# FFN up projection: one pass of 512 prompt tokens per Strassen half, sample tokens as separate float32 products

## The chip, the core and the metric

The kernel runs on one core of a Trainium2 chip. The metric is the device time of one execution in microseconds (us), the median of several runs. The core has five engines with instruction queues of their own: PE (matrix products; its weight loads are listed as PEld), DVE (vectors), ACT (activations, copies, casts), POOL (general) and SP (which here only issues DMA transfers). They meet through semaphores.

## The reference

The program is one step of an encoder layer for 1024 prompt tokens (one new stream) and 32 sample tokens (one running stream): a mixer of three head groups, its output projection, and a feed-forward network with a causal convolution. The change concerns the last:

```python
def conv_ffn(xn, buf, w_up, conv_w, conv_b, w_down):      # D_MODEL 1024, D_FF 2816, FFN_CONV 3
    up = xn @ w_up                                        # (T, 1024) @ (1024, 5632)
    up, buf = causal_dwconv(up, buf, conv_w, conv_b)      # per channel: b + sum_j up[t - 2 + j] * w[j]
    gate, val = jnp.split(up, 2, axis=-1)
    return (jax.nn.gelu(gate, approximate=True) * val) @ w_down, buf
```

It is run for the prompt with an empty buffer and for the samples with a cache of the last two rows of `up` (`cache_ffn_conv`, 2 x 5632); both return the last two rows of their `up` (outputs `p_fc` and `q_fc`). All is float32.

## The kernel before

The kernel goes through its stages in one program: mixer projections and heads, output projection, up projection, down projection, tail. A tile scheduler sets the order on each engine from the order of the code, from priorities (`tc.high_priority`) and from explicit rules (`tc.issue_after`). Names in traces are those of tiles without their number.

A float32 product is made of three products of reduced type (`mm3`, L100 to 103): each operand is split into a high half (`...h`, a cast on ACT) and a low half (`...l`, the difference on DVE), and PE adds high x high (L101), low x high (L102) and high x low (L103) in PSUM.

The up projection uses one level of Strassen's method in Winograd's form. The 1024 inputs are cut in two (four k tiles of 128 each), the tokens in two halves of 512 columns, and the 5632 outputs into 22 pairs of 128 rows (`f` and `22+f`). Seven products p1 to p7 make one pair: `PROD` names their operands, of which those on the weights' side (A11, A12, A22, S1 to S4) are made anew for each f in `up_operands`, and those on the activations' side (B11, B21, B22, T1 to T4) are made once in `col_operands` and stay in SBUF. One product is four k tiles times three matmuls, 12 matmuls; seven are 84.

A Strassen half holds 512 prompt tokens and 16 of the samples, 528 columns. PSUM's bank holds 512, so `SUBS` cuts it in two passes, s=0 of 272 columns and s=1 of 256: 168 matmuls per f. `up_block` issues one pass. It is a generator, advanced by `up_all`: p2 into bank `puy`; p1 into `pux`, p5 into `puw`, p4 into `puz`; p6 on top of `pux` and p3 on top of `puw`; p7 on top of `pux`. Between them ACT copies `pux` or `puw` out (`keep`, L1345: c1, c5, c6, c7) and DVE adds such a copy and a bank into the conv's input `uu` (`out`, L1350), in pieces given by `PIECES`. `uu` has 1060 columns: the two prompt halves with the samples between them, and gaps of two columns for the conv's history.

`up_finish` runs for the f before: POOL fills gaps, samples' cache and halo (L1403 to 1406), ACT applies the middle tap and the bias (L1407), DVE the other two taps, ACT the GELU, DVE the product, and SP stores the result to `h_d` in DRAM (L1413). `up_raw` (L1292) loads the weights `wu<j>r` of the next f. In the entry to this stage, f=0's first pass is interleaved with the output projection's last two tiles (`zp`, tiles 6 and 7), whose normalized and transposed result (`z`, `fxt`, `xg`) is the last part of T1 and B22 of the second half.

The down projection reads `h_d` tiles back as `ht` and multiplies the prompt's part by Strassen as well. The samples are multiplied apart in `sample_products` (L1530): float32 products without split, 32 sample columns as weights and 512 columns of the down weights moving, into one quarter of the partitions of a bank each.

## Time and profile before

| | us |
|---|---|
| runs | 1359.47, 1356.77, 1357.68; median 1357.68 |
| span of the profiled execution | 1355.3 |
| PE busy | 1310.8 |
| DVE, ACT, POOL busy | 1025.2, 709.8, 317.6 |

The profile gives the span from the first to the last instruction. What lies around the span is not in it; the three runs without profile are 1.5 to 4.2 us above it, the median 2.4. In the rows of a timeline the first number is the start and the second the duration, both in us; of pipelined matmuls the durations overlap, so the rate is read from the distance of the starts. A bracket at the end gives the idle time ahead of an instruction and what ended it.

### The profile page before, as it was taken

The page shows a single profiled execution, that of the slowest core. Times are in us where ns is not written, and L with a number is a line of the kernel's source. Part 1 is how long each engine was busy: PE and PEld are TensorE (multiplying, and loading weights), DVE is VectorE, ACT ScalarE, POOL GpSimd, SP SyncE. Part 2 cuts the span into 40 slices and gives each one's busy share as a digit, 9 for nine tenths or more (in the row PEclk, how much of TensorE's full clock was granted, in tenths as well). Part 3 has the DMA queues.
Part 4 walks back from the last instruction along what each step waited for, and adds up shares of the span by engine and source line. Part 5 has one row for each costly group of instructions (what it writes and reads, how often), then busy time and mean ns, then how long its engine had stood idle before and what let it go on. Part 6 is the DMA issues. An engine that isn't in the chain of part 4 may idle for free.

```text
span 1355.3 us, 29229 instructions
## 1 busy us (share of the span) xinstructions
PE 1310.8 (97%) x11472; PEld 1196.7 (88%) x11472; DVE 1025.2 (76%) x1921; ACT 709.8 (52%) x1362; POOL 317.6 (23%) x530
## 2 busy tenths in 40 slices
PE   6999999999999999999999999999999999999997
PEld 5999889998888887767899999999999996678885
DVE  5795649768598678876998888888888876499566
ACT  5555556555574555435654554545554545454552
POOL 4532303135032254213211212111111110010005
PEclk9999999999998989989999999999999999999998
DMA  9799778886879963454315457536455239645435
GB/s 342 241 358 363 265 244 258 278 281 211 292 230 308 336 201 125 142 182 103 128 48 188 134 133 189 134 111 180 120 147 154 82 127 397 254 161 146 141 102 124
DMA packets 126881, 269.72 MB, mean 199 GB/s; under 512 B 24167, under 2 KB 59143, under 8 KB 126663
## 3 DMA queue, kind: packets, MB, share of 16 engines
q1 hardware_dynamic: 113111, 244.78, 53.2%
q0 software_dynamic: 9120, 18.62, 7.3%
q10 hardware_dynamic: 4512, 4.46, 1.0%
q8 instruction: 90, 1.47, 0.5%
q14 instruction: 48, 0.39, 0.1%
HBM read 206.72 MB, written 86.18 MB: 216 GB/s over the span
## 4 chain that ended last, share of the span: by engine, by line
PE 63%; DVE 5%; DMA 3%; ACT 3%; issue 2%; POOL 1%; SPq 0%; DVEq 0%; POOLq 0%; ACTq 0%
PE pux L103 5%; PE pux L102 5%; PE pux L101 5%; PE puw L101 3%; PE puw L103 3%; PE puw L102 3%; PE q L101 3%; PE q L102 3%; PE q L103 3%; PE x L101 2%; PE x L102 2%; PE x L103 2%; PE puz L103 2%; PE puz L101 2%; PE puz L102 2%
## 5 line engine op out<-in xcount | busy, mean ns | idle before, releaser
L1409 DVE SCALAR_TENSOR_TENSOR y<-uu,fconv_sb,y 128x1060 f32<-128x1060 f32 x88 | 116.2, 1320 | 36.8 <-ACT y L1407 36.2
L1345 ACT COPY c<-pux 128x272 f32<-128x272 f32 (+1 forms) x132 | 49.3, 375 | 50.5 <-PE pux L103 49.8
L1407 ACT ACTIVATE y<-uu,fconv_sb 128x1060 f32<-128x1060 f32 x44 | 56.1, 1275 | 8.5 <-POOL uu L1403 7.8
L101 PE MATMUL pv<-wt_0h,xh 128*128 128x256 f32 (+1 forms) x192 | 56.3, 293 | 3.6 <-DVE xl L334 1.6
L103 PE MATMUL zp<-woh,cl 128*128 128x512 f32 (+1 forms) x144 | 57.7, 401 | 1.5 <-DVE cl L1106 1.5
L1406 POOL COPY fhalo<-uu 128x2 f32<-128x2 f32 x44 | 16.6, 376 | 180.7 <-DVE uu L1350 180.6
L101 PE MATMUL zp<-woh,ch 128*128 128x512 f32 (+1 forms) x144 | 57.8, 410 | 0.8 <-ACT ch L1105 0.8
L102 PE MATMUL zp<-wol,ch 128*128 128x512 f32 (+1 forms) x144 | 57.9, 402 | 0.0
L103 PE MATMUL pv<-wt_1h,xl 128*128 128x256 f32 (+1 forms) x192 | 55.1, 287 | 0.0
L103 PE MATMUL pv<-wt_0h,xl 128*128 128x256 f32 (+1 forms) x192 | 55.0, 286 | 0.0
L102 PE MATMUL pv<-wt_0l,xh 128*128 128x256 f32 (+1 forms) x192 | 54.8, 286 | 0.0
L101 PE MATMUL pv<-wt_1h,xh 128*128 128x256 f32 (+1 forms) x192 | 54.7, 285 | 0.0
L102 PE MATMUL pv<-wt_1l,xh 128*128 128x256 f32 (+1 forms) x192 | 54.4, 283 | 0.0
L1585 POOL TENSOR_TENSOR gss<-gss 128x1 f32<-128x1 f32 (+1 forms) x9 | 8.2, 906 | 185.0 <-ACT gjk L1578 185.0
L221 POOL TENSOR_SCALAR hrs<-hss 128x5 f32<-128x5 f32 (+3 forms) x27 | 10.1, 375 | 176.5 <-DVE hss L1015 172.6
L831 DVE COPY_PREDICATED P<-masks_sb,sc 128x352 f32<-128x352 int32 (+3 forms) x53 | 37.9, 715 | 5.9 <-PE sc L744 5.0
L101 PEld LDWEIGHTS pv<-wt_0h,xh 128*128 128x128 f32 x192 | 36.4, 190 | 5.3 <-DVE xl L334 2.1
L1403 POOL COPY uu<-uu 128x2 f32<-128x2 f32 x44 | 28.0, 637 | 38.8 <-DVE uu L1350 37.8
L101 PEld LDWEIGHTS pv<-wt_1h,xh 128*128 128x128 f32 x192 | 36.2, 189 | 0.7 <-issue 0.6
L222 POOL TENSOR_TENSOR hrs<-hrs,mhalf 128x5 f32<-128x5 f32 (+3 forms) x27 | 36.2, 1341 | 2.2
L103 PEld LDWEIGHTS pv<-wt_0h,xl 128*128 128x128 f32 x192 | 36.5, 190 | 0.2
L102 PEld LDWEIGHTS pv<-wt_0l,xh 128*128 128x128 f32 x192 | 36.5, 190 | 0.1
(1743 smaller groups left out, 5321.0 us busy)
## 6 DMA issues: line engine op xcount, KB each, us to landing
wrP<-in_w_dn SPq DMA_DIRECT2D x27, 512.0 KB, 4.4
h_d<-y SPq DMA_DIRECT2D x22, 530.0 KB, 3.7
ht<-h_d SPq DMA_DIRECT2D x22, 530.0 KB, 10.5
wt_0r<-in_w_tok SPq DMA_DIRECT2D x21, 512.0 KB, 5.7
wt_1r<-in_w_tok SPq DMA_DIRECT2D x21, 512.0 KB, 6.3
ws_d<-in_w_dn POOLq DMA_DIRECT2D x20, 512.0 KB, 8.9
wrP<-ws_d SPq DMA_DIRECT2D x20, 512.0 KB, 4.0
wt_0l<-lt_d SPq DMA_DIRECT2D x14, 512.0 KB, 4.5
```

Source lines behind the costliest of these rows:

```text
L101: pe.matmul(ps, lh[0], rh[0], start=first, stop=False, **kw)
L102: pe.matmul(ps, lh[0], rh[1], start=False, stop=False, **kw)
L103: return pe.matmul(ps, lh[1], rh[0], start=False, stop=last, **kw)
L221: pool.tensor_scalar(out, ss, 1.0 / width, eps, op0=ALU.mult, op1=ALU.add)
L222: pool.tensor_tensor(out, out, mhalf[:n, :cols], op=ALU.pow)
L831: dve.copy_predicated(dst, mk.broadcast_to([n, 11, *mk.shape[2:]]), src)
L1345: kept[name] = act.copy(t, ps)
L1403: pool.tensor_copy(u[:, GAP_P:GAP_P + 2], u[:, GAP_S - 2:GAP_S])
L1406: behind["POOL"] = pool.tensor_copy(fhalo[:, j, :], u[:, NCOL - 2:NCOL])
L1407: act.activation(y, u, AF.Identity, scale=fconv[:, j, 2:3], bias=fconv[:, j, 3:4])
L1409: dve.scalar_tensor_tensor(y, uu[i][:, s:s + NCOL], fconv[:, j, s:s + 1], y, op0=ALU.mult, op1=ALU.add)
L1585: pool.tensor_tensor(ss[:n, 0:1], ss[:n, 2:3], ss[:n, 3:4], op=ALU.add)
```

## The change

- `SUBS`, `PIECES` and the gaps go. Only f=0 still runs in two passes (0 and 1, both of 256 columns, as the second needs the last out-projection tiles). From f=1 to f=21 there is one pass of 512 columns, so 84 matmuls instead of 168. The activation halves (`X`) are one set of tiles, 512 columns wide; T2, T3 and T4 live in pool `px1`, the rest in `px0`. In the last f the order of products is p2, p5, p1, p3, p6, p4, p7 in code.
- `uu`, `y`, `h_d` and `ht` have 1024 columns. `out` is one DVE sum of 512. Of the POOL copies only `fhalo` remains.
- The samples get a second layout of the up weights, `w_us`, made on the host: 24 rounds (3 groups of columns x 8 k tiles), each [128, 4 (in the last group 3 used), 512]. `up_samples` is a generator that `up_all` advances behind p4 of f=1 and later. A round is 4 or 3 float32 matmuls (weights 32 sample columns, moving 512 columns of `wus`) into quarters of one bank `us`. After 8 rounds ACT copies the bank to SBUF, PE transposes it in four steps, and ACT puts the parts into `smp_u` [128, 44, 34]. Behind the last group POOL does the conv of the samples (12 operations of 128x704), ACT the GELU, POOL the product into `smp_h`, which `sample_products` uses in place of `ht`.
- `wus` holds two rounds (1 MB each) in the SBUF place of `xg0`; a round's reload is issued when it has been used. The samples' cache is read straight into `smp_u` (pieces of 8 bytes) and `q_fc` written from it.
- The program is built with a DMA scratch of 4096 bytes instead of the default.

```diff
-SUBS = [(0, 272), (272, 256)]
+NU = 2 * NF
+UGROUPS = [(0, 4), (4, 4), (8, 3)]
...
     def halves(name, src):
             if name not in res:
-                p = pool_[name in ("T2", "T3")]
-                h = p.tile([128, 4, n], F32R, name=f"{name}h{s}")
...
+                p = pool_[name in ("T2", "T4", "T3")]
+                res[name] = tuple(p.tile([128, 4, 512], F32R, name=f"{name}{x}") for x in "hl")
+            h, l = (t[:, :, at] for t in res[name])
...
     def up_block(pw_, f, s, W, X, uu, own={}):
-        n = SUBS[s][1]
+        at = slice(0, 512) if s is None else slice(256 * s, 256 * s + 256)
+        n = at.stop - at.start
...
         def out(i, j, x, ps, op=ALU.add):
-            for (a0, a1, c) in PIECES[j, s]:
-                dve.tensor_tensor(uu[i][:, 2 + c:2 + c + a1 - a0], x[:, a0:a1], ps[:, a0:a1], op=op)
+            c = 2 + 512 * j + at.start
+            dve.tensor_tensor(uu[i][:, c:c + n], x, ps, op=op)
...
-            pool.tensor_copy(u[:, GAP_P:GAP_P + 2], u[:, GAP_S - 2:GAP_S])
-            pool.tensor_copy(u[:, GAP_S:GAP_S + 2], fcache[:, j, :])
-            pool.tensor_copy(fcache[:, j, :], u[:, GAP_P - 2:GAP_P])
...
+    def up_samples():
...
+        def load(i):
+            if i < len(ROUNDS):
+                g, k = ROUNDS[i]
+                nq = UGROUPS[g][1]
+                sp.dma_start(wus[:, i % 2, :nq], a["w_us"][8 * g + k, :, :nq])
+        smp_u = own.tile([128, NU, 2 + DEC], F32, name="smp_u")
+        sp.dma_start(smp_u[:, :, 0:2], a["fcache"])
...
+        sp.dma_start(smp_x, xn_d[:, :, SEQ:])
...
+        for g, (c0, nq) in enumerate(UGROUPS):
+            ps = psf.tile([128, 512], F32, tag="sx", name=f"us{g}", bufs=1)
+            for k in range(8):
+                for q in range(nq):
+                    pe.matmul(ps[DEC * q:DEC * q + DEC], smp_x[:, k, :], wus[:, i % 2, q, :], start=k == 0, stop=k == 7)
+                load(i + 2)
+                i += 1
+                if k < 7:
+                    yield
+            m = DEC * nq
+            us = own.tile([128, 512], F32, tag="us", name=f"usr{g}", bufs=1)
+            act.copy(us[:m], ps[:m])
+            yield
+            tp = psb.tile([128, 4, 128], F32, tag="big", name=f"ust{g}", bufs=3)
+            for b in range(4):
+                pe.transpose(tp[:, b, :m], us[:m, 128 * b:128 * b + 128], ident[:m, :m])
+            for b in range(4):
+                act.copy(smp_u[:, 4 * c0 + b:4 * (c0 + nq):4, 2:2 + DEC], tp[:, b, :m].rearrange("p (q t) -> p q t", t=DEC))
...
     def up_all(pw_, W0, X, uus, py, freed, ahead, begun):
-            for s in range(2):
+            for s in (0, 1) if f == 0 else (None,):
...
                 yield
+                while f and n_rounds < f * 28 // 18:
+                    next(rounds, None)
+                    n_rounds += 1
                 next(blk)
...
-                    pe.matmul(ps[r:r + DEC], hts[q + NP * k][:, SMP:SMP + DEC], wraws["P2" if k else "P1", q][:, j],
+                    pe.matmul(ps[r:r + DEC], smp_h[:, q + NP * k, :], wraws["P2" if k else "P1", q][:, j],
```

On PE, in the steady part of the stage, before (f=4; p4 ends in `puz4_0`, p6 follows; further on p3 ends and the second pass begins with `puy4_1`):

```order
L102 MATMUL puz4_0_10020<-T4l0_8847,A22_4h_9841 128x272
L103 MATMUL puz4_0_10020<-T4h0_8846,A22_4h_9841 128x272
L101 MATMUL pux4_0_10018<-T2h0_8842,S2_4h_9850 128x272
L102 MATMUL pux4_0_10018<-T2l0_8843,S2_4h_9850 128x272
...
L103 MATMUL puw4_0_10019<-B22h0_8835,S4_4h_9854 128x272
L101 MATMUL puy4_1_10115<-B21h1_8948,A12_4h_9835 128x256
```

The same place on PE after (`us0` is the bank of the first group of columns; x8 are two rounds of four):

```order
L89 MATMUL puz4_None_9687<-T4l_8928,A22_4h_9585 128x512
L90 MATMUL puz4_None_9687<-T4h_8927,A22_4h_9585 128x512
L1433 MATMUL us0_9448<-wus_8941,smp_x_9300 32x512 x8
L88 MATMUL pux4_None_9685<-T2h_8923,S2_4h_9594 128x512
L89 MATMUL pux4_None_9685<-T2l_8924,S2_4h_9594 128x512
```

The rounds stand between p4 and p6, and there is no second pass. Such an insertion comes once in each f from 1 to 17, 17 in all; f=1, 4, 6, 8, 9, 11, 13 and 15 hold two rounds, the others one, and one round is cut into 3 matmuls in f=2 and 1 in f=3. The three groups of transposes stand ahead of the rounds of f=7 and f=12 and shortly behind the round of f=17.

On ACT, in the entry, before (`xg` filled from the last transposes, then casts of the first half, with the out-projection's `z6` and its sums between):

```order
L1258 CAST B11h_8813<-xg_6906 128x1088
L1210 ACTIVATE xg_6906<-fxt_8705,gcols_sb 128x128 x4
L1210 ACTIVATE xg_6906<-fxt_8714,gcols_sb 128x128 x4
L1130 ACTIVATE z_8747,oss_8632<-zp_8633 128x512
L1130 ACTIVATE z_8747,oss_8632<-zp_8634 128x512
L1258 CAST B22h_8835<-xg_6906 128x1088
L1258 CAST T1h_8831<-xg_6906 128x1088
```

The same place on ACT after:

```order
L1117 ACTIVATE z_8743,oss_8632<-zp_8633 128x512
L1117 ACTIVATE z_8743,oss_8632<-zp_8634 128x512
L1242 CAST B21h<-xg_6885 128x4x256
L1242 CAST B11h<-xg_6885 128x4x256
L1242 CAST B22h<-xg_6885 128x4x256
L1118 COPY z_8743<-zp_8633 128x512
```

The casts of B21 and B11 of the first half have moved behind the filling of `xg` and the two activations of `z6`.

On SP, ahead of the weights of f=2, before:

```order
L1185 DMA x_d<-xr_8752 128x1024
L1805 DMA fconv_sb<-in_fconv 128x176
L1807 DMA fcache_sb<-in_fcache 128x88
L1185 DMA x_d<-xr_8807 128x1024
L1292 DMA wu2r<-in_w_up 128x1024
L1292 DMA wu24r<-in_w_up 128x1024
```

The same place on SP after:

```order
L1172 DMA x_d<-xr_8803 128x1024
L1418 DMA wus<-in_w_us 128x2048 x2
L1421 DMA smp_u<-in_fcache 128x44x2
L1424 DMA smp_x<-xn_d 128x8x32
L1276 DMA wu2r<-in_w_up 128x1024
L1276 DMA wu24r<-in_w_up 128x1024
L1418 DMA wus<-in_w_us 128x2048 x2
L1407 DMA h_d<-y_9211 128x1024
```

Four loads for the samples now stand ahead of `wu2r`, and the reload of the first two rounds stands ahead of the store of the first `h`.

More of the change, by code (lines that the diff above doesn't have):

```diff
@@ L1323, in body, with product @@
     done = [None]
-    def product(ps, p, W, X, first, last):
+    def product(ps, p, W, X, first, last, at):
         (wh, wl), (xh, xl) = W[PROD[p][0]], X[PROD[p][1]]
@@ L1864, in body @@
     p4s.close()
+    pgs.close()
 def _layout(i):
```

209 lines of the change are left out of this document (117 added, 92 removed).

## The prediction

> **What bounds the kernel now.** I read the page's busy times first, then the chain that ended last, then a table of windows by stage, and last the timelines of the matmuls themselves.
>
> ```profile
> PE 1310.8 (97%) x11472; PEld 1196.7 (88%) x11472; DVE 1025.2 (76%) x1921; ACT 709.8 (52%) x1362; POOL 317.6 (23%) x530
> PE 63%; DVE 5%; DMA 3%; ACT 3%; issue 2%; POOL 1%; SPq 0%; DVEq 0%; POOLq 0%; ACTq 0%
> ...
> 657.50:690.00 32.50, 28.80 (x211) 28.22 (x210) 30.62 (x46) 20.64 (x32) 9.54 (x15) 0.89 0.18 58
> 700.00:800.00 100.00, 100.00 (x820) 100.00 (x819) 84.08 (x141) 51.08 (x88) 16.58 (x45) 1.00 0.52 151
> 1140.00:1200.00 60.00, 58.19 (x271) 39.17 (x270) 31.60 (x51) 25.54 (x49) 0.00 (x0) 1.00 0.76 288
> ```
>
> The window rows give bounds and length, then busy time of PE, PEld, DVE, ACT and POOL, the granted clock, the DMA share and GB/s. In the steady up projection (700 to 800) PE is busy for the whole window at full clock. No other engine is: DVE has 84.08, ACT 51.08, DMA 0.52. So a microsecond taken from PE's issue there is a microsecond off the end, until DVE's share binds. The entry into the stage (657.5 to 690) is another matter: PE has 28.80 of 32.50, the clock is 0.89, and DVE with 30.62 is the fullest engine.
>
> **Term 1, long passes.** Per f-tile, 84 matmuls of 272 columns and 84 of 256 become 84 of 512; this holds for f=1 to 21. First the rate before, by one POOL instruction that comes once per f-tile, by the change-over of shapes in the last f-tile, and then the rate of 512-column matmuls of the same three-pass form in the down projection (one P7h cast per 12 of them) and in the output projection.
>
> ```profile
> 727.93 0.58 POOL L1406 COPY fhalo<-uu 128x2 f32<-128x2 f32 x1 [4.96 <-DVE uu L1350]
> ...
> 789.54 0.58 POOL L1406 COPY fhalo<-uu 128x2 f32<-128x2 f32 x1 [4.98 <-DVE uu L1350]
> ...
> 1108.26 0.29 PE L101 MATMUL pux<-T3h,S_21h 128*128 128x272 f32 x1
> ...
> 1109.77 0.28 PE L101 MATMUL pux<-B11h,A_21h 128*128 128x256 f32 x1
> ...
> 1111.20 0.28 PE L101 MATMUL puw<-T1h,S_21h 128*128 128x256 f32 x1
> ...
> 1296.35 0.62 ACT L107 CAST P7h<-ht 128x512 fp32r<-128x512 f32 x1 [1.58 <-PE x L103]
> ...
> 1301.79 0.62 ACT L107 CAST P7h<-ht 128x512 fp32r<-128x512 f32 x1 [1.58 <-PE x L103]
> ...
> 651.64 0.39 PE L101 MATMUL zp<-woh,ch 128*128 128x512 f32 x1
> ...
> 653.00 0.39 PE L101 MATMUL zp<-woh,ch 128*128 128x512 f32 x1
> ```
>
> Three f-tiles take 789.54 − 727.93 = 61.61 us, so one takes 20.54, and a pair (272 and 256) 20.54/84 = 244.5 ns. By shape: 12 of 272 take 1109.77 − 1108.26 = 1.51, or 125.8 ns each; 12 of 256 take 1.43, or 119.2. The 512 form takes (1301.79 − 1296.35)/24 = 226.7 ns, and (653.00 − 651.64)/6 = 226.7 in the output projection. Sixteen columns cost 6.6 ns, so 256 cost about 106 and each matmul carries some 13 ns whatever its width; the long pass pays that once instead of twice and drops 16 columns. Saved: 244.5 − 226.7 = 17.8 ns a pair, 1.495 us an f-tile, **−31.4 us** for 21. For f=0 the passes stay at two but the first loses 16 columns: 84 × 6.6 ns = **−0.55**.
>
> The Trainium skill ("TensorE: Matmul & The Clock Gate", section "Back-to-back issue gap") puts an isolated warm matmul at N/2.4 + 2.5 ns. By it 272 and 256 would take 225.0 ns and 512 would take 215.8, a saving of 9.2 ns a pair and 16.2 us in all. The trace's 119.2 for 256 columns lies 10 ns above that rule's 109.2, and here the measurement decides.
>
> **Term 2, sample rounds.** The 32 sample tokens leave the passes and come back as 24 rounds of 4 (16 rounds) or 3 (8 rounds) float32 matmuls, 32 sample columns stationary, 512 weight columns moving, each into its quarter of PSUM's partitions. The down projection has exactly this form, four at a time (x8, as each float32 matmul leaves two records) and once two at a time (x4).
>
> ```profile
> 1125.85 0.39 PE L103 MATMUL q<-P2w,P2h 128*128 128x512 f32 x1
> 1126.17 1.07 PE L1530 MATMUL s<-wrP,ht 128*32 128x512 f32 x8
> 1127.17 0.50 PE L101 MATMUL q<-P2w,P2h 128*128 128x512 f32 x1
> 1127.51 0.39 PE L102 MATMUL q<-P2w,P2h 128*128 128x512 f32 x1
> ...
> 1194.07 0.39 PE L103 MATMUL x<-P1w,P1h 128*128 128x512 f32 x1
> 1194.39 1.05 PE L1530 MATMUL s<-wrP,ht 128*32 128x512 f32 x4
> 1195.37 0.50 PE L101 MATMUL q<-P4w,P4h 128*128 128x512 f32 x1
> 1195.71 0.39 PE L102 MATMUL q<-P4w,P4h 128*128 128x512 f32 x1
> ```
>
> From the last ordinary matmul to the second one behind the group it is 1127.51 − 1125.85 = 1.66; two ordinary intervals would be 0.45, so a group of four costs 1.21 us. A group of two costs 1195.71 − 1194.07 − 0.45 = 1.19: the quarters run beside each other, and three cost what four do. Of the 1.21, 1.00 (1126.17 to 1127.17) is the round and 0.2 the change of form on both sides. PE's order has 17 insertions, always behind product p4; eight hold two rounds, one round is cut into 3 and 1 over two f-tiles, so there are 25 round times. 17 × 1.20 + 8 × 1.00 = **+28.4**. No row shows two rounds in a row on the same quarters. Ends: 25 × 1.00 = 25.0 if the changes of form hide; 25 × 1.21 = 30.3 if a second round pays its own. I take 28.4, since the change of form is at the border.
>
> **Term 3, transposes.** Each of three groups is brought back with four 128x128 float32 transposes. The nearest row is such a group inside the output projection:
>
> ```profile
> 640.50 0.39 PE L103 MATMUL zp<-woh,cl 128*128 128x512 f32 x1
> 640.73 0.60 PE L1101 MATMUL ctp<-ident,cat 128*128 128x128 f32 x4
> 641.09 0.48 PE L101 MATMUL zp<-woh,ch 128*128 128x512 f32 x1
> 641.40 0.40 PE L102 MATMUL zp<-wol,ch 128*128 128x512 f32 x1
> ```
>
> 641.40 − 640.50 − 0.45 = 0.45, times three is **+1.35**.
>
> **Term 4, the entry.** Here the order of the activation halves changes.
>
> ```profile
> 676.05 0.58 PE L101 MATMUL puw<-T1h,S_0h 128*128 128x256 f32 x1 [2.93 <-ACT T1h L1258]
> 676.43 0.43 PE L101 MATMUL pux<-B11h,A_1h 128*128 128x272 f32 x1
> ...
> 679.15 0.41 PE L102 MATMUL puw<-T1l,S_0h 128*128 128x256 f32 x1
> ...
> 681.50 0.41 PE L101 MATMUL pux<-T2h,S_0h 128*128 128x256 f32 x1
> ...
> 682.68 0.39 PE L101 MATMUL puw<-B22h,S_0h 128*128 128x256 f32 x1 [0.77 <-ACT c L1345]
> ...
> 693.74 0.33 SPq L1292 DMA_DIRECT2D wu2r<-in_w_up  x1
> ...
> 697.35 0.62 ACT L107 CAST A_2h<-wu2r 128x512 fp32r<-128x512 f32 x1 [0.73 <-DMA wu2r<-in_w_up]
> ```
>
> Before, PE loses 2.93 and 0.77 to waits, and behind the first it runs slow: 12 of 272 take 2.72 instead of 1.51 and 11 of 256 take 2.35 instead of 1.31, another 2.25. Together 5.95 us. The last prompt tile's normalization on ACT and POOL, with DVE's copies and sums, feeds T1h there, and nothing of that chain is shortened. After, ACT runs the out-projection's z6 ahead of the first half's B21h and B11h, T2 and T4 of that half come later on DVE, and p6 of f=0 has to wait for its T2 low half; against that, p1 of f=1 fills the gap before T1 with 12 matmuls of 512 instead of 272 (2.72 against 1.51 at full clock). Walked with the durations of these rows: T1's second half comes about 1 us later (677 instead of 676.05), because z7's chain starts 1 us later on ACT; the filler does 1.2 us more work ahead of it; the rest of f=0 behind T1 is the same work at the same slow start. That is −0.2. The wait of p6 for T2 is about 2.7 us at a place where PE ran on before; the wait for T1 comes after it and would have been idle anyway, so it swallows that but for 0 to 2 us. I take **+0.4** in all, near the low end, as the swallowing is exact if T1 really ends last. The outer ends are −5.95 (all of the loss gone) and +5.2 (one more wait of 2.93 with its slow 2.25).
>
> **What I cost at nothing.** Per f-tile DVE has 0.84 × 20.54 = 17.3 us and ACT 10.5; both fit into the 19.04 us of 84 × 226.7 ns even unchanged, and they shrink (four 512-wide sums for twelve pieces, 66 copies for 132, y of 1024 for 1060). If DVE did not keep up, PSUM banks would come free late and PE would wait at p6. The three gap copies on POOL go; the samples' convolution there is 13 instructions of 704 columns, due four f-tiles (76 us) after the last round, which covers even 5 us each. The second weight layout brings 16 × 1.05 + 8 × 0.79 = 23 MB in 330 us, 70 GB/s on 151: a share near 0.76, as the 1140 window has with PE at 58.19 of 60. Each reload waits in SP's queue until PE has read its buffer, and the store of h and the weights of the f-tile after next stand behind it; those have most of a period. The down projection's h tiles get 3.4% smaller; PE misses only 1.81 of 60 there, so I count no gain.
>
> **Sum.** −31.4 − 0.55 + 28.4 + 1.35 + 0.4 = −1.8 us. On the profiled span of 1355.3 that is 1353.5. The median of the runs, 1357.68, lies 2.4 above that span; I take the same distance: **1355.9 us**. About 0.2% (2.7 us) is what a measurement can tell from no change.
>
> **Rivals.**
> - *Entry smooth.* p1 of f=1 covers the wait, so the clock never drops: 5.95 + 0.4 less, 1349.5. For it: the longer filler. Against: T1h hangs on DVE, 30.62 of 32.50 busy. Chance 0.13.
> - *Rounds at 1.00.* Term 2 is 25.0: 1352.5. For it: the x4 group costs as much as the x8, so there is idle array time; against: the 0.50 record and late successor stand behind every group. Chance 0.12.
> - *A longer entry (slower).* The wait at p6 or T1 reaches 2.93 again a second time: +5.2 on a sum without the 0.4, 1360.7. It decides once the entry loses 4.5 us beyond my sum. For it: ACT and DVE run late by their new order. Chance 0.12.
> - *Weights of f=2 late.* SP now sends 2 MB of sample weights, the sample cache as 5632 pieces of 8 bytes and the sample columns ahead of wu2r, which already lands 0.73 us late. Whole-run, one queue's row bounds such pieces:
>
> ```profile
> q10 hardware_dynamic: 4512, 4.46, 1.0%
> fcache_sb<-in_fcache SPq DMA_DIRECT2D x1, 44.0 KB, 2.9
> ```
>
> 1.0% of 16 × 1355.3 us over 4512 packets is 48 ns each; 5632 of them over 16 engines take 17 us, while the same bytes in whole rows landed in 2.9. Begun near 680, where the entry's last casts run, the long end pushes wu2r some 4 us back: 1360. Chance 0.07.
> - *Rounds wait for their weights.* Half a microsecond at each of 17 insertions: 1364. Against: two buffers and about 19 us a period. Chance 0.05.
> - *The long pass saves half.* If the fixed part per matmul did not shrink in this stage, where PEld shows 100.00 of 100, 15.7 us are missing: 1371.6. Both stages with 512 columns speak against it. Chance 0.04. The skill's rule above would end here, near 1371.
>
> **Numbers.** The forecast keeps 0.47, its own range 1353.5 to 1358.5. Faster by over 2.7 (below 1355.0): 0.13 of the forecast, with both first rivals nearly whole, 0.37. Slower (above 1360.4): three quarters of the longer entry, half of the late weights, the last two, 0.20. Same: 0.43. The range 1350.5 to 1362 leaves out half of the smooth entry and the last two.
>
> **What would show it.** Period of the fhalo copy 19.04 us in f-tiles without a round, 20.2 with one, 21.2 with two; ordinary matmuls 227 ns apart; about 1.2 us around each single round, 2.2 around a double one; no PE wait on wus, DVE under 85% between 700 and 1080; entry idle on PE of 3 to 5 us ending on T1 or T2 halves. I am wrong if the passes are not at 227 ns, if a round's quarters run one after another (4 us, +70), or if wu2r lands after 700.

## The result, and the profile after

| | before | after |
|---|---|---|
| median of 4 runs each, us | 1357.22 | 1398.62 |
| profiled execution, span | 1355.3 | 1401.4 |

The ratio is 1.0314 (95% interval 1.0282 to 1.0345): 3.1% slower, where 1355.9 was forecast. The page of the changed kernel, its busy times and the shares of the chain that ended last:

```profile
PE 1324.7 (95%) x9896; PEld 1103.0 (79%) x9896; DVE 1014.0 (72%) x1748; ACT 693.8 (50%) x1294; POOL 310.5 (22%) x411
...
PE 57%; DVE 8%; DMA 7%; ACT 3%; issue 2%; POOL 1%; SPq 0%; DVEq 0%; POOLq 0%; ACTq 0%
```

PE has 1576 records fewer and yet 14 us more busy time, and DMA's share of the chain has gone from 3% to 7%. Windows of two stretches (bounds, length, busy time and count of PE, PEld, DVE, ACT, POOL, then granted clock, DMA share, GB/s) tell where to look:

```profile
760.00:1030.00 270.00, 270.00 (x1231) 205.59 (x1231) 210.69 (x258) 125.98 (x191) 43.70 (x52) 1.00 0.77 210
1050.00:1100.00 50.00, 28.56 (x118) 22.59 (x117) 22.19 (x23) 11.66 (x20) 15.13 (x11) 0.80 0.76 43
```

The steady part is as forecast: PE full, clock 1.00, DVE at 78%, DMA at 0.77. At the end of the stage PE has 28.56 of 50, while the DMA engines are busy for a share of 0.76 and move only 43 GB/s. PE's waits between 640 and 1170 (engine, tile, line, releaser: total, times, longest):

```profile
PE puy_None L88 <- ACT A_19h L94: 20.6, 1, 20.6
PE pux L89 <- DVE T2l L1243: 3.2, 1, 3.2
PE pux L88 <- ACT c L1329: 2.6, 1, 2.6
PE pux_None L88 <- ACT c_21None L1329: 2.2, 1, 2.2
```

One wait of 20.6 us for the cast of `wu19r`, the weights of f=19, is half of the loss. The timelines of SP and of PE around it:

```profile
1051.91 0.65 SPq L1447 DMA_DIRECT2D out_q_fc<-smp_u  x1
1053.96 9.30 SPq L1276 DMA_DIRECT2D wu19r<-in_w_up  x1
...
1086.12 0.80 PE L88 MATMUL puy_None<-B21h,A_19h 128*128 128x512 f32 x1 [20.63 <-ACT A_19h L94]
```

SP stores `q_fc` (5632 pieces of 8 bytes) directly ahead of these weights; issuing `wu19r` takes 9.30 us instead of the usual 0.33, and behind the wait PE runs at the low clock (matmuls 0.43 us apart) until 1091.25. The view of the DMA engines from 1020 to 1085, busy tenths and GB/s in 40 slices of 1.6 us:

```profile
DMA  6999910082791079910043899994999578299954
GB/s 47 189 166 188 319 59 0 0 204 119 285 308 68 0 66 174 330 76 0 0 7 5 3 2 2 3 1 0 14 21 23 28 30 33 30 53 139 58 40 149
```

From the 21st slice (1052) to the 36th the engines move 0 to 53 GB/s, and in the 23rd to 27th they are 80% to over 90% busy at 1 to 3 GB/s. That is the look of small pieces: time without bytes.

The rest is smaller and spread. The table measures stages on PE: from the last output-projection matmul (zp) to the first T1 matmul of f=2, from there to the same matmul of f=17, and so on, then to the first P2 matmul and the end. "Forecast" is before plus the terms of the prediction, with its own round times (1.20 us, and 1.00 for a second round); "mended" is e8, an experiment below.

| us | before | forecast | after | mended (e8) |
|---|---|---|---|---|
| zp to T1 of f=2 | 52.92 | 55.8 | 63.08 | 61.39 |
| f=2 to f=17 | 308.22 | 311.5 | 314.82 | 311.07 |
| f=17 to 18 | 20.52 | | 20.92 | 20.65 |
| f=18 to 19 | 20.53 | | 43.16 | 19.40 |
| f=19 to 21 | 41.05 | | 35.99 | 35.36 |
| f=21 to P2 | 16.12 | | 20.61 | 17.39 |
| P2 to end | 238.41 | 238.4 | 241.83 | 236.52 |
| zp to end | 697.8 | 696.0 | 740.4 | 701.8 |

(The marker in f=2 lies 24 long matmuls into that f-tile, 2.4 us more work than the 24 of 272 columns before; the forecast of the first row counts this, and what is behind f=17 has as much less. From f=17 on f-tiles overlap differently before and after, so only the sums compare there. zp itself ends between 653.6 and 662.3 in runs whose work up to there is the same.)

### The profile page after: what moved, and what is told of

Same layout as the page of the kernel before. It is cut to its first block, busy times and chain, and to the rows that moved or that the text cites. A ratio compares the mean times of both kernels' runs of the same rounds, so it can differ in the third digit from the quotient of the medians.

```text
span 1401.4 us, 25578 instructions
## 1 busy us (share of the span) xinstructions
PE 1324.7 (95%) x9896; PEld 1103.0 (79%) x9896; DVE 1014.0 (72%) x1748; ACT 693.8 (50%) x1294; POOL 310.5 (22%) x411
## 4 chain that ended last, share of the span: by engine, by line
PE 57%; DVE 8%; DMA 7%; ACT 3%; issue 2%; POOL 1%; SPq 0%; DVEq 0%; POOLq 0%; ACTq 0%
PE pux_None L88 4%; PE pux_None L90 4%; PE pux_None L89 4%; PE q L88 3%; PE q L89 3%; PE q L90 3%; PE puw_None L89 3%; PE puw_None L88 3%; PE puw_None L90 3%; PE x L88 2%; DMA wu19r<-in_w_up 2%; PE x L89 2%; PE x L90 2%; PE us L1433 2%; PE zp L88 1%
## 5 line engine op out<-in xcount | busy, mean ns | idle before, releaser
L1403 DVE SCALAR_TENSOR_TENSOR y<-uu,fconv_sb,y 128x1024 f32<-128x1024 f32 x88 | 116.0, 1318 | 23.3 <-ACT y L1401 22.9
L88 PE MATMUL pv<-wt_0h,xh 128*128 128x256 f32 (+1 forms) x192 | 55.8, 291 | 4.2 <-DVE xl L321 1.6
L1401 ACT ACTIVATE y<-uu,fconv_sb 128x1024 f32<-128x1024 f32 x44 | 54.8, 1245 | 6.3 <-DVE uu L1334 5.1
L1006 POOL TENSOR_TENSOR cat<-cat,gt 128x320 f32<-128x320 f32 (+3 forms) x27 | 31.3, 1160 | 26.1 <-DVE cat L1004 25.9
L90 PEld LDWEIGHTS pv<-wt_1h,xl 128*128 128x128 f32 x192 | 36.3, 189 | 0.3
L89 PEld LDWEIGHTS pv<-wt_1l,xh 128*128 128x128 f32 x192 | 36.3, 189 | 0.1
```

The costliest lines, as they stand in the source:

```text
L88: pe.matmul(ps, lh[0], rh[0], start=first, stop=False, **kw)
L89: pe.matmul(ps, lh[0], rh[1], start=False, stop=False, **kw)
L90: return pe.matmul(ps, lh[1], rh[0], start=False, stop=last, **kw)
L1006: pool.tensor_tensor(cat[:n, c0:c0 + 64 * nh], cat[:n, c0:c0 + 64 * nh], gt[:n, c0:c0 + 64 * nh], op=ALU.mult)
L1401: act.activation(y, u, AF.Identity, scale=fconv[:, j, 2:3], bias=fconv[:, j, 3:4])
L1403: dve.scalar_tensor_tensor(y, uu[i][:, s:s + SEQ], fconv[:, j, s:s + 1], y, op0=ALU.mult, op1=ALU.add)
```

## The experiments

Times are medians beside runs of the kernel before on the same chip; "base" is the kernel to which the edit is made.

| run | base | edit | median, us | ratio to before (95%) |
|---|---|---|---|---|
| e1_store | after | q_fc stored from one piece | 1371.99 | 1.0123 (1.0099 to 1.0148) |
| e2_align | after | T2 to T4 moved by 32 bytes | 1395.20 | 1.0302 (1.0279 to 1.0326) |
| e3_read | after | sample cache read in one piece | 1395.22 | 1.0297 (1.0273 to 1.0320) |
| e4_actq | after | q_fc stored from ACT's queue | 1394.69 | 1.0301 (1.0274 to 1.0328) |
| e5_px1 | e1 | T2 to T4 to offset 0 | 1366.83 | 1.0081 (1.0050 to 1.0112) |
| e6_shift | e1 | weight halves to offset 32 | 1368.78 | 1.0102 (1.0068 to 1.0136) |
| e7_ph | e1 | down projection's halves to offset 0 | 1367.47 | 1.0088 (1.0057 to 1.0120) |
| e8_all | e1 | e5, e7, and the first down casts later | 1359.54 | 1.0025 (1.0006 to 1.0043) |
| e10_pairs | e8 | all rounds in pairs | 1359.17 | 1.0048 (1.0029 to 1.0067) |
| e11_norounds | e8 | one round of eight | 1340.22 | 0.9899 (0.9879 to 0.9920) |
| e12_norm7 | e8 | last tile's norms left out | 1356.61 | 1.0016 (1.0002 to 1.0030) |
| e13_order | e10 | entry: residual ahead of T2, T4 | 1357.12 | 1.0022 (1.0009 to 1.0036) |
| e14_noT2 | e8 | entry: no wait for T2 | 1355.96 | 1.0001 (0.9985 to 1.0016) |
| e15_t2first | e8 | entry: T2 first | 1355.87 | 1.0012 (0.9999 to 1.0025) |

### The store of q_fc: e1 and e4

e1 copies the two columns on POOL and stores one contiguous row per partition:

```diff
-        sp.dma_start(a["q_fc"], smp_u[:, :, DEC:DEC + 2])
+        q_fc = own.tile([128, NU, 2], F32, name="q_fc")
+        pool.tensor_copy(q_fc, smp_u[:, :, DEC:DEC + 2])
+        sp.dma_start(a["q_fc"], q_fc)
```

> The samples' last two rows of up (q_fc) are first copied on POOL into a contiguous tile of 88 columns and stored as 128 pieces of 352 bytes instead of 5632 pieces of 8 bytes; nothing else changes. Theory (the pieces hold up SP's rings, and wu19r stands behind them): the 20.6 us wait of puy on A_19h goes, with some 2.6 us of slow clock behind it; about 1375. Rival (the weights of f=19 are late because SP's queue is behind with the reloads of the sample rounds): the wait stays within 3 us of 20.6; about 1398.

Measured: 1371.99, some 23 us below e2, e3 and e4, which keep the store. f=18 to 19 takes 19.37 instead of 43.16, and PE has no wait for A_19h. SP's timeline:

```profile
1046.82 0.34 SPq L1449 DMA_DIRECT2D out_q_fc<-q_fc  x1
1048.75 0.33 SPq L1276 DMA_DIRECT2D wu19r<-in_w_up  x1
```

The weights issue in 0.33 again. The store's pieces are the cause of the stall; 23.8 us is its price, 20.6 of wait and the rest mostly the low clock behind it. e4 leaves the pieces and moves the store to ACT's queue:

```diff
-        sp.dma_start(a["q_fc"], smp_u[:, :, DEC:DEC + 2])
+        act.dma_start(a["q_fc"], smp_u[:, :, DEC:DEC + 2])
```

> The q_fc store with its 5632 pieces is issued from ACT's queue instead of SP's. If the pieces only stand ahead of wu19r on SP's rings, the wait at f=19 goes: about 1375, like the staged store. If the DMA engines themselves are held by the pieces, wu19r takes its share beside them and the wait shrinks to about half, 8 to 12 us: about 1387. If ACT's own queue stalls at the issue, as SP's did for 9.3 us, PE waits for c copies instead, some 5 us.

Measured: 1394.69, nothing gained. The timelines, and the share of the queues between 1040 and 1076 (q10 is ACT's, q1 SP's):

```profile
1043.51 0.64 ACTq L1447 DMA_DIRECT2D out_q_fc<-smp_u  x1
1045.56 0.33 SPq L1276 DMA_DIRECT2D wu19r<-in_w_up  x1
1077.48 0.62 ACT L94 CAST A_19h<-wu19r 128x512 fp32r<-128x512 f32 x1 [25.53 <-DMA wu19r<-in_w_up]
...
q10 hardware_dynamic: 5648, 0.05, 60.4%
q1 hardware_dynamic: 257, 0.94, 40.7%
```

`wu19r` is issued at once and still lands 32 us later. 60.4% of 16 engines over 36 us is 348 us of engine time, 62 ns a piece on average, and the two queues fill the engines. None of the three expected outcomes came (all of the wait gone, half of it gone, or ACT's own queue held at the issue, which took 0.64 us). So the issuing queue was not what held the weights; the 16 DMA engines were. The Trainium skill says so ("DMA: Bandwidth & Descriptors", section "Issuing engines are not separate DMA queues"): issuing from several engines saves the issuers' time alone; the trace agrees: PE still waits 21.1 us, where it waited 20.6.

### The read of the sample cache: e3

```diff
-        sp.dma_start(smp_u[:, :, 0:2], a["fcache"])
+        fc = own.tile([128, NU, 2], F32, name="fc")
+        sp.dma_start(fc, a["fcache"])
+        pool.tensor_copy(smp_u[:, :, 0:2], fc)
```

> The samples' cache is read into a contiguous tile (128 pieces of 352 bytes) and copied into smp_u on POOL, instead of 5632 pieces of 8 bytes. Theory (the read holds smp_x and wu2r up on SP, as smp_x is issued 13.7 us behind it): wu2r is issued at about the time of before plus 3, A_2h no longer waits 2.95 us, and the entry gains 2 to 4 us; about 1395. Rival (the entry is late by the chain through POOL to T1 alone): PE reaches f=2 at the same time within 1 us; 1398.

In the kernel after, the read stands ahead of `smp_x` and `wu2r` in SP's queue:

```profile
685.49 0.57 SPq L1421 DMA_DIRECT2D smp_u<-in_fcache  x1
699.19 0.53 SPq L1424 DMA_DIRECT2D smp_x<-xn_d  x1
702.72 0.33 SPq L1276 DMA_DIRECT2D wu2r<-in_w_up  x1
```

`wu2r` is issued 41.7 us after zp there, 38.8 in e2, 38.9 in e4, and 38.9 in e3, where the pieces are gone. So the pieces of the read do not hold it. What does is `smp_x` ahead of it, which waits for a low half on DVE in both kernels (SP's waits, of after and of e3):

```profile
SPq L1424 <- DVE T3l L1243: 13.1, 1, 13.1
SPq L1426 <- DVE T3l L1243: 13.4, 1, 13.4
```

ACT's first cast of `wu2r` waits 2.99 us in e3 as in e2 (2.95 in after), f=2 is reached 60.22 us after zp in e3, 59.98 in e2 and 60.24 in e4, and PE shows no wait for these weights in any of them. The theory fails, and the rival's "same time within 1 us" is what came. The read is also short. SP's queue between 684 and 692 of after (packets, MB, share of 16 engines):

```profile
q1 hardware_dynamic: 5649, 0.05, 38.5%
```

38.5% of 16 engines over 8 us is 49 us, 8.7 ns a piece; a piece of the store took 62 ns on average. That is not the price of sharing the engines: between 1050 and 1056 of e4 they moved 1643 pieces of the store and one packet of another load, 58 ns a piece. The same number of pieces of the same size cost seven times as much in the store as in the read; no run here shows why, nor why the store's rate changes on its way (in after 14 GB/s in its first 1.5 us, then 1 to 4).

### Where the operands lie: e2, e5, e6, e7

In the kernel after, the distance of product starts is not the same for all operands. PE's timeline, the first of each group of 12 matmuls in the f-tile after a round:

```profile
1027.87 0.39 PE L88 MATMUL puw_None<-B22h,S_16h 128*128 128x512 f32 x1
...
1030.61 0.39 PE L88 MATMUL puy_None<-B21h,A_17h 128*128 128x512 f32 x1
...
1033.33 0.40 PE L88 MATMUL pux_None<-T3h,S_16h 128*128 128x512 f32 x1
...
1036.14 0.40 PE L88 MATMUL pux_None<-B11h,A_17h 128*128 128x512 f32 x1
```

12 matmuls with B21 take 2.72 us (226.7 ns each), 12 with T3 2.81 (234). Removing the gaps and the `fcache` tile had shifted addresses in SBUF: as the programs are built, all these operands lay at multiples of 128 bytes before; after, T2, T3 and T4 (pool `px1`) lie 32 bytes past one, and so do the activations' halves P1h to P7h of the down projection, whose 32-byte `pad` had suited 1060 columns. Edits, of e2, e5, e6 and e7 in this order:

```diff
-    p7.tile([128, 8], F32, name="pad1")
...
-    p7.tile([128, 8], F32, name="pad1")
+    p7.tile([128, 16], F32, name="pad1")
...
     p0 = p4s.enter_context(tc.tile_pool(name="p4r", bufs=1, side="left", reuse_waits="tile"))
+    p0.tile([128, 8], F32, name="pad0")
...
-        ph[0].tile([128, 8], F32, name="pad")
```

> The 32-byte pad ahead of pool px1 is left out, so that T2, T4 and T3 begin at a multiple of 64 bytes instead of 32 beyond one. Theory (a moving operand of 512 columns that starts 32 bytes off costs 6.9 ns more a matmul): p6, p4 and p7 go from 232.7 to 233.6 ns to 226.7; 36 x 6.6 ns x 21 f-tiles = 5 us less, about 1393.5. Rival (those products run beside DVE and ACT work that slows them): intervals stay at 233, time unchanged.

> On top of the staged q_fc store (1372), the pad ahead of pool px1 is 64 bytes instead of 32, so that T2, T4 and T3 begin at a multiple of 128 bytes, as the weight halves do that they meet on PE. Theory (what counts is the distance between the two operands' addresses within 128 bytes; 32 apart cost 6.9 ns a matmul, 64 apart half of it): p6, p4 and p7 fall to 226.7 ns, about 6 us less, 1366. Rival (any multiple of 64 is as good as another, and the rest is work beside them): as with the pad left out, 229.3 to 230.4 ns, 1369.

> On top of the staged q_fc store, 32 bytes are put ahead of the weight halves, which moves them, B and T1 to 32 beyond a multiple of 128, where T2, T4 and T3 are already, and the stationary halves of the down projection to 64 beyond, against 32 for its moving ones. Theory (distance): all seven up products at 226.7 ns, the down projection stays at 233; about 1366. Rival (each operand must itself start at a multiple of 64 or 128): all seven up products at 233 or more, the down projection no better; about 1377 or more.

> On top of the staged q_fc store, the 32-byte pad at the head of the down projection's pool is left out; its stationary halves then begin at a multiple of 128 as its moving ones do. Theory (distance): its 924 matmuls of 512 columns go from 233.3 to 226.7 ns, 6 us less, 1366, and the up projection stays as it was. Rival (the down projection is slower for another reason, the smaller h tiles or the samples' own tile): 233 stays, 1372.

Measured, as mean distance of starts between 760 and 1030 (and in the down projection), with the address past a multiple of 128 bytes:

| kernel | T2, T3, T4 at | weight halves at | T3, ns | B21, ns | P.h at (P.w at 0; e6: 32) | down, ns |
|---|---|---|---|---|---|---|
| after | 32 | 0 | 233.6 | 226.7 | 32 | 233.3 |
| e2 | 64 | 0 | 230.4 | 226.7 | 32 | 233.3 |
| e5 | 0 | 0 | 226.7 | 226.7 | 32 | 233.3 |
| e6 | 32 (B also) | 32 | 226.6 | 226.6 | 64 | 233.3 |
| e7 | 32 | 0 | 233.6 | 226.7 | 0 | 226.7 |

e6 is the run that decides: there everything lies 32 bytes off, and everything runs at 226.6. It is the distance between the moving and the stationary operand within 128 bytes that counts, not the address of either: 32 bytes apart cost 6.9 ns a matmul, 64 about half. (e2 was to bring T2 to T4 to 226.7 or leave them at 233; at a distance of 64 it did neither.) The same stretch in e6:

```profile
1020.53 0.39 PE L88 MATMUL puy_None<-B21h,A_17h 128*128 128x512 f32 x1
...
1023.25 0.39 PE L88 MATMUL pux_None<-T3h,S_16h 128*128 128x512 f32 x1
...
1025.97 0.39 PE L88 MATMUL pux_None<-B11h,A_17h 128*128 128x512 f32 x1
```

Here each takes 2.72. In the down projection of e5 (`pad` kept) 12 matmuls on P7h take 2.80 (1289.60 to 1292.40), in that of e7 (`pad` gone) 2.72 (1295.11 to 1297.83). By stage: f=2 to 17 takes 314.84 in e1 and 311.07 in e5 and e6; P2 to the end 241.85 in e1 and 236.47 in e7. In whole runs the intervals of e1, e5, e6 and e7 touch each other, so these sizes rest on the stages and not on the medians.

### All mends, and the last f-tile: e8

In e1, PE waits at f=21 for a copy of `pux`. ACT's timeline there:

```profile
1124.85 0.62 ACT L94 CAST P2h<-ht 128x512 fp32r<-128x512 f32 x1 [8.77 <-DMA ht<-h_d]
1125.37 0.58 ACT L1329 COPY c_21None<-pux_None 128x512 f32<-128x512 f32 x1
```

The copy stands behind a cast of the down projection, and that waits for `ht` from DRAM. e8 has the edits of e5 and e7, and puts the cast behind the last such copy:

```diff
-        for p in range(1):
-            begun["P2", p] = down_operands(ph[0], "P2", p, True)
+        with tc.issue_after(kept["c6"].ins):
+            begun["P2", 0] = down_operands(ph[0], "P2", 0, True)
```

> The staged q_fc store, both alignments (T halves and the down projection's at multiples of 128), and the down projection's first casts on ACT put behind the copy c6 of the last f-tile, so that p7 does not wait for a copy that stands behind a cast which waits for a DMA. Theory: 1372 less 6, 6 and some 3 us (the wait of 2.2 and the slow clock behind it): 1357. Rival (the casts behind c6 delay the first product of the down projection by as much): 1360.

Measured: 1359.54, ratio 1.0025. PE's wait at c_21 falls to 0.7 and f=21 to P2 to 17.39, and the down projection does not get longer for it (236.52, e7 236.47), so the rival's delay did not come. The size of the gain is open: e1 takes 20.69 from f=21 to P2, but e5 and e7, which also lack this edit, take 18.97 and 18.65. They wait there too (2.34 and 1.76), but in e1 the matmuls behind the wait run 0.43 us apart for some 3 us and in e5 they do not. What is left above the forecast is the entry: 61.39 instead of 55.8 in this profile.

### The rounds: e10 and e11

```diff
-                while f and n_rounds < f * 28 // 18:
+                while f and n_rounds < 1 + 2 * (f * 13 // 17):
```

> On top of e8_all (1359.5) the rounds of the samples are taken two at a time, in 13 insertions instead of 17. Theory (an insertion costs 0.2 us of change of form beside its rounds, a second round behind the first only 0.87): 4 to 5 insertions fewer and no cut round, about 2.5 us less, 1357. Rival (two rounds an f-tile double the traffic of the sample weights in those f-tiles, 2 MB in 21 us, and a reload comes late): PE waits on wus, 1360 or more.

```diff
-                for q in range(nq):
-                    pe.matmul(ps[DEC * q:DEC * q + DEC], smp_x[:, k, :], wus[:, i % 2, q, :], start=k == 0, stop=k == 7)
+                for q in range(nq if k == 0 else 0):
+                    pe.matmul(ps[DEC * q:DEC * q + DEC], smp_x[:, k, :], wus[:, i % 2, q, :], start=True, stop=True)
```

> On top of e8_all, of the samples' 24 rounds only the first of each group is computed (the sample outputs are then incomplete); all loads, transposes and the conv stay. Theory (the rounds cost PE 27 us, as the trace reads, and nothing else waits on them): some 22 us less, 1337.5, which is the 18 us below before that the long passes alone would have brought. Rival (part of the rounds lay under other waits): under 18 us less, 1342 or more.

e10 gained nothing that shows, and PE does not wait for `wus` as its rival had it: f=17 to 18 fell from 20.65 to 19.43, and f=18 to 19 rose from 19.40 to 21.50. PE's waits of e10 between 990 and 1080 (e8 has none in that stretch), and one DVE sum with the POOL instruction beside it:

```profile
PE pux_None L88 <- ACT c_18None L1329: 1.1, 1, 1.1
PE puy_None L88 <- ACT A_19h L94: 0.8, 1, 0.8
...
1044.40 2.04 POOL L1457 TENSOR_TENSOR smp_y<-smp_y,smp_y 128x704 f32<-128x704 f32 x1
...
1044.91 2.09 DVE L1302 TENSOR_TENSOR wu18r<-wu18r 128x512 f32<-128x512 f32 x1
```

The same sum in e8, where it comes ahead of POOL's convolution of the samples:

```profile
1036.79 0.69 DVE L1302 TENSOR_TENSOR wu18r<-wu18r 128x512 f32<-128x512 f32 x1
```

Beside POOL's 704-column instructions DVE's sums of two SBUF tiles take two to four times as long, in e8 (2.62 us for one at 1053.30) as in e10; a sum with one input in PSUM keeps its 0.68 there (e8, 1048.02). With a round fewer in front, PE reaches this stretch 1.2 us sooner and finds DVE and, behind it, ACT late: the gain turns into a wait. The prediction had the convolution on POOL "covered"; it is, but it costs DVE time.

e11 took 19.95 us less than e8 from f=2 to 17, where 19 of 21 rounds are gone: 1.05 each with their change of form. So PE's time for the rounds is real and does not hide. In the whole run less came of it, 17.8 us from zp to the end and 17 by the ratios, just under the rival's 18: the entry takes 63.44, and at the one round in it PE lost 2.3 us to no wait that the profile names.

### The entry: e12, e13, e14, e15

In the entry of after, PE waits here:

```profile
670.41 0.38 PE L89 MATMUL pux<-T2l,S_0h 128*128 128x256 f32 x1 [3.16 <-DVE T2l L1243]
...
677.68 0.39 PE L88 MATMUL pux<-T3h,S_0h 128*128 128x256 f32 x1 [2.65 <-ACT c L1329]
...
680.04 2.21 PE L1194 MATMUL fxt<-ident,z 128*128 128x128 f32 x12
...
686.48 0.39 PE L88 MATMUL puw<-T1h,S_0h 128*128 128x256 f32 x1 [1.06 <-ACT T1h L1242]
```

The stage varies. All times in the table are in us after the last zp matmul: the start of the first T1 matmul of f=0's second half, for which PE waits in the last row above, and of T1 of f=2. Beside them stand PE's waits between zp and T1 of f=2, added up, and the granted clock there.

| run | T1 of f=0 | T1 of f=2 | PE's waits | clock |
|---|---|---|---|---|
| before | 18.52 | 52.92 | 3.70 | 0.94 |
| after | 25.49 | 63.08 | 7.80 | 0.92 |
| e8 | 25.55 | 61.39 | 7.98 | 0.94 |
| e1, e5, e7, e10 | 22.48 to 22.54 | 58.61 to 58.82 | 6.73 to 6.78 | 0.97 |
| e2, e3, e4, e6 | 22.43 to 22.53 | 59.98 to 60.24 | 6.52 to 6.66 | 0.94 |
| e12 | 22.35 | 59.74 | 6.42 | 0.94 |
| e13 | 21.47 | 58.99 | 5.86 | 0.94 |
| e14 | 20.33 | 57.16 | 4.38 | 0.97 |
| e15 | 20.34 | 56.23 | 6.27 | 1.00 |

In the changed kernel and the runs up to e10 the work between zp and T1 of f=2 is the same. Two things differ: the clock, and in after and e8 T1 comes 3 us later. The second goes with one POOL instruction on a single column, part of tile 7's norm, in after and in e1:

```profile
672.28 3.27 POOL L208 TENSOR_SCALAR oss<-oss 128x1 f32<-128x1 f32 x1 [5.61 <-ACT z L1175]
```

```profile
671.11 1.00 POOL L208 TENSOR_SCALAR oss<-oss 128x1 f32<-128x1 f32 x1 [5.59 <-ACT z L1175]
```

The same form takes 0.19 where DVE is idle. It reaches PE through ACT, where the copy `c` that p7 waits for stands behind `z` (after):

```profile
676.22 1.15 ACT L1178 ACTIVATE z<-xr,oss 128x1024 f32<-128x1024 f32 x1 [4.02 <-POOL oss L209]
677.27 0.35 ACT L1329 COPY c<-pux 128x256 f32<-128x256 f32 x1
```

The edits:

```diff
# e12: tile 7's scales come from a constant, POOL's part is left out
+        if u != 7:
             pool.tensor_tensor(ss[:n, 2:3], ss[:n, 0:1], ss[:n, 1:2], op=ALU.add)
             rstd_of(ss[:n, 3:4], ss[:n, 2:3], n, 1, 1024)
...
# e13: T2's low half, T4's sum behind tile 7's residual sum, T4's cast behind z7's square
+                if s == 0 and name == "T4":
+                    late.enter_context(tc.issue_after(kept["z"].ins))
                 act.copy(h, src)
+                if s == 0 and name == "T2":
+                    late.enter_context(tc.issue_after(kept["x7"].ins))
...
# e14: p6 of f=0, first half, uses B22's halves in place of T2's
+        if f == 0 and p == "p6" and at == slice(0, 256):
+            X = {**X, "T2": X["B22"]}
...
# e15: T2's low half ahead of tile 7's scaling on DVE, its cast ahead of z6's square on ACT
+                with tc.issue_after(kept["T2"][1].ins):
                     dve.scalar_tensor_tensor(pss[hf], pss[hf], ss[:, 3:4], gm[:, cs[hf]], op0=ALU.mult, op1=ALU.mult)
...
+        with tc.issue_after(kept["T2"][0].ins) if u == 6 else ExitStack():
             act.activation(z[:n], x[:n], AF.Square, accum_out=ss[:n, 0:1])
```

> On top of e8_all, the output projection's last tile is scaled by a constant instead of its two reciprocal roots, so the five POOL instructions of that tile are left out (the last 128 prompt tokens come out differently). Theory (T1 of the second half ends the entry, and it is late by POOL's steps, which take 2.6 and 1.5 to 3.8 us beside a busy DVE): T1's second half comes 4 to 5 us earlier and the time falls by 3 us or more, 1356. Rival (DVE's queue with T2, T4 and T3 ends it): less than 1 us.

> On top of e10_pairs, three rules put the last output-projection tile ahead of the first half's T operands: T2's low half and T4's sum on DVE behind that tile's residual sum, T4's cast on ACT behind that tile's square. Theory (T1 ends the entry): its chain starts 1 to 2 us earlier; 1 us less than e10_pairs. Rival (T2's low half, 0.7 us later, ends it): 0 to 1 us more.

> On top of e8_all, p6 of f=0's first half takes the halves of B22 in place of T2 (the first 256 prompt tokens then come out differently); T2 is still made. The wait for T2's low half, 3.2 us, is so taken away, and nothing else. Theory (the waits of the entry add up, since the last transposes that feed T1 stand in PE's own queue behind the products that wait): from the end of the output projection to T1 of f=2 it takes 3 to 5 us less than the 58.6 to 61.4 of the runs so far, 1355.5. Rival, the step of the prediction (the wait for T1 comes last and swallows it): the wait moves to T1, less than 1 us gained, 1359.

> On top of e8_all, T2's cast on ACT goes ahead of z6's square and its low half on DVE ahead of the last output-projection tile's scaling; all is computed. Theory (the waits add up): T2's wait falls under 0.7 us, the chain to T1 starts 1.2 us later without mattering, and the entry gains 2 to 4 us: 1356. Rival (the chain through the last tile ends the entry): what T2 gains, T1 loses, within 1 us of e8_all.

e12: without tile 7's norm T1 comes at 22.35, hardly earlier than the 22.5 of the runs in which POOL's column is short. So there tile 7's norm is not what T1 waits for, and the theory's 4 to 5 us did not come. e13: with tile 7 ahead T1 starts 1.06 us earlier, as its theory had it, but the wait for T2's low half grows to 3.75 and f=2 is reached at 58.99, beside 58.61 in e10. From zp to the end e13 takes 699.9 and e10 699.6; the difference of their medians lies ahead of this stage.

e14: without the wait for T2, T1 starts 2.2 us earlier than in e1, and f=2 is reached 1.5 to 1.7 us earlier than in the four runs at the same clock. That is more than the rival's 1 and less than the theory's 3 to 5. (Its median holds another 1.2 us: one insertion of rounds fewer, f=2 to 17 in 309.86.)

e15: PE's waits in f=0's first half, and for T1:

```profile
660.98 0.39 PE L89 MATMUL pux<-T2l,S_0h 128*128 128x256 f32 x1 [0.25 <-DVE T2l L1245]
...
666.90 0.39 PE L89 MATMUL puz<-T4l,A_0h 128*128 128x256 f32 x1 [1.46 <-DVE T4l L1245]
...
674.81 0.39 PE L88 MATMUL puw<-T1h,S_0h 128*128 128x256 f32 x1 [1.06 <-ACT T1h L1244]
```

T2's wait falls from 3.16 to 0.25, and T1 again starts 2.2 us earlier. But waits for T4 (0.96 and 1.46) come up in its place, and the sum of the waits is only 0.5 below that of e1 (POOL's column took 2.12 here). The 56.23 rests on two other things: the clock stays at 1.00 through the whole entry, and six of the eight round matmuls of f=1 now come behind T1 of f=2, which is 0.87 us (f=2 to 17 takes 311.97 instead of 311.07). What e15 gains at f=2 is therefore no proof that the waits add.

What both runs show is that T1 is not independent of the wait for T2: it starts 2.2 us earlier when that wait goes, with nothing taken from tile 7's own work. The reason is in the first fence: the transposes `fxt`, from which T1 is made, start without a wait of their own. They stand in PE's queue behind p6 and p7, and what PE loses there delays T1, which was to swallow it. So the early wait adds to the late one in part.

e15 is the best complete version found: same as before (1.0012, 0.9999 to 1.0025; 697.4 from zp to the end, before 697.8), not faster. A version that beats both was not found.

## Why the prediction was wrong

Of zp to the end the prediction expected 696.0 and the trace of after has 740.4. The difference of 44.4 us, by the stages of after against e8 (for the entry against the forecast): the store of q_fc 23.8; the entry 7.3 (63.08 − 55.8); the down projection's operands 5.3 (241.83 − 236.52); the up projection's 4.6 (f=2 to 21, without the stall); the last f-tile 3.2 (in part the clock, see e8). That is 44.2.

- **What bounds the kernel, Term 1 (long passes): right, on operands that lie alike.** (One reading was off: beside PE, the weight loads, PEld, filled the window from 700 to 800 as well. In after they fill 205.59 of 270, while PE stays full.) With e5's offsets all seven products run at 226.7 ns and f=2 to 17 takes 311.07 where the terms give 15 × 19.04 + 25.0 + 0.9 = 311.5. The rival that the long pass saves half did not come, and neither did the 215.8 ns that the prediction worked out, as an estimate, from the Trainium skill's "Back-to-back issue gap" ("TensorE: Matmul & The Clock Gate"); the trace has 226.7. (25.0 is 15 × 1.20 + 7 × 1.00.) What failed is the transfer of that number to every operand: the change also moved addresses, and for T2, T3 and T4 it is 234.
- **Term 2 (rounds): right, slightly high.** Around a single and around a double round:

```profile
1023.66 0.40 PE L90 MATMUL puz_None<-T4h,A_16h 128*128 128x512 f32 x1
1023.98 1.06 PE L1433 MATMUL us<-wus,smp_x 128*32 128x512 f32 x6
1024.97 0.50 PE L88 MATMUL pux_None<-T2h,S_16h 128*128 128x512 f32 x1
1025.31 0.39 PE L89 MATMUL pux_None<-T2l,S_16h 128*128 128x512 f32 x1
...
770.44 0.40 PE L90 MATMUL puz_None<-T4h,A_4h 128*128 128x512 f32 x1
770.77 1.92 PE L1433 MATMUL us<-wus,smp_x 128*32 128x512 f32 x16
772.62 0.50 PE L88 MATMUL pux_None<-T2h,S_4h 128*128 128x512 f32 x1
772.96 0.39 PE L89 MATMUL pux_None<-T2l,S_4h 128*128 128x512 f32 x1
```

  1025.31 − 1023.66 − 0.45 = 1.20 as forecast; 772.96 − 770.44 − 0.45 = 2.07, so a second round is 0.87 and not 1.00, and the term 17 × 1.20 + 8 × 0.87 = 27.4 instead of 28.4. No round waited for its weights.
- **Term 3 (transposes): right**, 0.53 a group instead of 0.45.
- **Term 4 (entry): wrong.** The step that failed is the place of T1. The prediction walked it to 677, 1 us later than before (19.5 us after zp), and let it swallow p6's wait for T2. The T2 wait came, larger than the 2.7 put there (3.16), and a wait for `c` with it; T1 hangs on the transposes behind both and came at 22.5, in after at 25.5. Without the T2 wait (e14, e15) it comes at 20.3, within 0.8 us of the walk. f=2 is reached 2.8 to 4.4 us above the forecast where POOL's column is short, 7.3 in the profile of after. So the rival of a longer entry (+5.2) came as well.
- **What was costed at nothing: wrong, and the largest step.** It left the store of q_fc out. The rival on late weights had counted the pieces of the read, at 48 ns each, and the diff stores as many. In the read a piece took 8.7 ns and nothing waited for it; in the store it took 62 ns, with the weights of f=19 right behind: 23.8 us. "No gain" in the down projection was wrong twice over: with its operands alike it takes 1.9 us less than before (236.52 against 238.41), as the change left it 3.4 more.
- **Weights of f=2 late: came, by another cause and without a price.** `wu2r` was issued at 702.72, later than the 700 that was to prove the forecast wrong, and PE did not wait for it. The pieces of the read were not what held it (e3).

What stays open: why POOL's column took 3.27 us in some executions and 1.00 in others, and with it 3 us of T1's start. In after it ends with DVE's last sum (675.55 and 675.50), in e1 at the border of two sums (672.11 and 672.06), but no run isolates that. Open too: why the same wait is followed by slow matmuls in one execution and not in another, which moves the entry and the last f-tile by 1 to 2 us, and why a stored piece costs so much more than a read one. The smaller DMA scratch was part of every run of the changed kernel and was not tried apart.

## What to carry to other kernels

Price every transfer in pieces as well as in bytes, the stores too, and read what stands behind it in time: a store of 5632 pieces of 8 bytes held all DMA engines for over 20 us and cost 24 us, while a read of as many was over in 3. Another queue did not help, one copy ahead of the store did. Before a late transfer is put down to the one ahead of it, look at what its queue waits for. An edit that removes or resizes a tile moves the addresses behind it, so before a rate is carried from one product to another, compare the operands' offsets. And a late wait swallows an early one only if what it waits for is not made from work that stands in the waiting engine's own queue.

## What the runs showed of the hardware

- Matmuls of 512 float32r columns run 226.7 ns apart with both operands at the same offset within 128 bytes, 233 to 234 with 32 bytes between them, about 230 with 64 (e2, e5, e6, e7). Only these three distances were tried.
- An 8-byte piece took, on average, 62 ns of a DMA engine in the store of e4 and 8.7 ns in the read of after. Beside the store the large transfers had 40.7% of the engines' time and moved 0.94 MB in 36 us. The Trainium skill's "Specifications" (page "DMA: Bandwidth & Descriptors") has transfers below 512 bytes do a read-modify-write; no run here shows that step, only the price.
- DVE and POOL slow each other: a 512-column DVE sum took 2.09 us instead of 0.69 beside POOL's two-input instructions (e10), while a sum with one input in PSUM kept its 0.68 beside such an instruction (e8), and a POOL instruction on one column 3.27 instead of 0.19 while DVE summed SBUF tensors back to back (after). The Trainium skill ("GPSIMD Engine Reference", section "Specifications") has POOL share its SBUF interface with DVE and contend with DVE instructions of two SBUF inputs; these rows agree.
- Two rounds of quarter-width float32 matmuls in a row cost 0.87 us for the second, and three quarters cost what four do (1.20 with the change of form).
- A wait of 2.24 us on PE was followed, 1 us later, by some 3 us of matmuls 0.43 us apart (e1, f=21, granted clock 0.59 in that stretch); a wait of 2.34 at the same place was not (e5, clock 1.00).
